# Output tiles of two channel mixers in pairs by seven block products, and a token-major end, in a two-layer hybrid trunk on one core

## The chip, the cores and the metric

The kernel runs on one core of one Trainium2 chip. The metric is the device time of one execution in microseconds (us); lower is better. Before the change it is 1336.59 us, the median of 3 runs (1335.65 to 1339.41).

## What is computed

The reference is a trunk of two layers over 512 tokens of width 1024 with 256 memory tokens. Layer 0 mixes time with a recurrence, layer 1 with attention over chunks; both add memory attention, an output projection, and then a channel mixer. At the end the stream is normalised once more. The change touches the channel mixers (`conv_glu`) and the last line:

```python
def conv_glu(h, w_in, conv_w, conv_b, w_out):
    gate, val = jnp.split(h @ w_in, 2, axis=-1)
    gp = jnp.pad(gate, ((0, 0), (CONV_W - 1, 0), (0, 0)))
    conv = conv_b + sum(conv_w[j] * gp[:, j:j + seq] for j in range(CONV_W))
    return (jax.nn.gelu(conv, approximate=False) * val) @ w_out
...
    x = x + conv_glu(rms_norm(x, ln2[layer]), ffn_in[layer], ffn_conv[layer], ffn_conv_b[layer], ffn_out[layer])
return rms_norm(x, ln_f)
```

`w_in` is 1024 by 5632, `w_out` 2816 by 1024, all in float32.

## The kernel before, in words

**Layout.** The stream lies transposed in SBUF: `xT[:, m]` is the m-th of 8 tiles of 128 features (partitions) by 512 tokens. Each float32 operand of a dense product is split into a high part of type fp32r and the rest (`whi`, `wlo` of a weight, `r1h`, `r1l` and so on of an activation), and a product is three matmuls: high by high and high by low with the same weights (lines 201 and 202), and low weights by high activations (line 206). `dense` runs all matmuls of the first two kinds, then all of the third.

**Channel mixer, in part (`ffn`).** 22 hidden tiles, each with a gate and a value output. Fourteen of them go by `seven`: the two outputs by the two token halves, with the 8 k tiles in two groups of 4, form a product of two-by-two blocks, which takes seven block products instead of eight. One block product (`prod`, lines 418, 419 and 421) is 12 matmuls of 128 by 256. The left blocks are `wv`, `w1`, `wy`, `wx` (sums and differences of weights, made on VectorE and split again); the right blocks are two plain ones (`B`) and four sums of blocks of the activations (`T`), made once per layer by `sums` and kept in `xh` (high) and `tl` (low). The eight other tiles go by `eight`: two dense products of 8 k tiles, 512 tokens wide.

**Channel mixer, out part.** A loop over the 8 output tiles m. The weights of a tile come in three pieces of 8, 7 and 7 k tiles (`load_w`, line 183: a DMA into `wraw`; line 172: the cast to `whi` on ScalarE; line 178: the rest into `wlo` on VectorE). `dense` runs 66 matmuls of 512 into one of two `psd` banks. Then VectorE multiplies by `rho`, the row of 1/rms (line 499), adds to `xT` (line 500), and `after` squares the tile, adds to `acc` and, in layer 0, writes the tile scaled and split into `r2h` and `r2l` for the next layer.

**Buffers.** `wraw` has 2, `whi` and `wlo` have 3 each. The hidden tiles 0 to 7 lie in `h_`, `l_` (`r1h`, `r1l` in layer 0; `r2h`, `r2l` in layer 1), 8 to 21 in `f3h`, `f3l`. The input of the mixer lies in the other pair, `ih`, `il`.

**The end (`finish`).** The last output tile runs in two token halves. While the second half is on TensorE, the first is finished: `norm_rho` sums squares by matmuls with a column of ones (line 251), takes the inverse root on VectorE (lines 225 to 229), spreads it over 128 columns (line 259), transposes that (line 262), copies it out (line 263), and two multiplications of 4 tiles by 256 tokens (line 1346) are stored feature-major (line 1348). The second half then goes through the same steps with nothing beside it.

**Order of the work.** A scheduler places each engine's instructions at build time, by the order of the code and when buffers come free; on the chip each engine runs its list in that order. SP issues most loads and the stores, POOL the loads that add to what is there (`accum_op`) and the loads of `xT`.

Of the kernel before, what the change touches and what calls it, by code (L numbers as in the profile page):

```python
# [18 lines left out]
P = 128  # L19
# [93 lines left out]
def trunk_kernel(ctx, tc, A, out):  # L113
# [39 lines left out]
    def ps_f(shape=(P, S)):  # L153
        return banks["F"].tile(list(shape), F32, name="psf", tag="psf")
# [8 lines left out]
    def tmp(dt=F32, shape=(P, S)):  # L163
        return banks["tmp"].tile(list(shape), dt, name="tmp", tag="tmp")
# [52 lines left out]
    def split_to(h_, l_, src):  # L217
        SC.copy(h_, src)
        V.tensor_tensor(l_, src, h_, op=ALU.subtract)  # L219
# [25 lines left out]
    def norm_rho(acc_, rho_, n=4, rc_=None):  # L245
        run(norm_steps(acc_, rho_, n, rc_))
# [103 lines left out]
    def ffn(l, hp, ih, il, h_, l_, xT, after, last=None):  # L350
# [8 lines left out]
        tl = hp.tile([P, 6, S], F32R, name="tl")  # L359

        def low(k, n):
            return tl[:, 2 * k + n] if k < 3 else (f3h, f3l)[n][:, NFF - 9]

        def high(k):
            return xh[0][:, 2 * k:2 * k + 2]

        xh = []

        def B(r, c):
            return lambda k: (ih[:, 4 * r + k, HT[c]], il[:, 4 * r + k, HT[c]])  # L370

        def T(n):
            n -= 1
            return lambda k: (high(k)[:, n // 2, HT[n % 2]], low(k, n // 2)[:, HT[n % 2]])

        def sums(k):
            u, w = tmp(), tmp()
            for t_, q in ((u, k), (w, k + 4)):
                nc.sync.dma_start(t_[:], xd[q])
                SC.activation(t_[:], t_[:], AF.Copy, scale=Vc(f"ln2_{l}", q))  # L380
            t12, t34 = tmp(), tmp()
            V.tensor_tensor(t12[:, HT[0]], u[:, HT[1]], u[:, HT[0]], op=ALU.subtract)
            V.tensor_tensor(t34[:, HT[0]], w[:, HT[1]], u[:, HT[1]], op=ALU.subtract)
            V.tensor_tensor(t12[:, HT[1]], w[:, HT[1]], t12[:, HT[0]], op=ALU.subtract)
            V.tensor_tensor(t34[:, HT[1]], w[:, HT[0]], t12[:, HT[1]], op=ALU.subtract)
            for n, t_ in enumerate((t12, t34)):
                split_to(high(k)[:, n], low(k, n), t_[:])

        def gated(j, g, v):
            c = tmp()  # L390
# [40 lines left out]
        def seven(j):  # L431
# [3 lines left out]
            nc.sync.dma_start(rg[:], A["ffn_in"][l, j, 0])  # L435
            GP.dma_start(rg[:, one], A["ffn_in"][l, j, 0][:, two], accum_op=ALU.add)
            nc.sync.dma_start(rv[:], A["ffn_in"][l, j, 1])
            wv = split_w(rv[:], 1024)
            w1 = split2(own("w1", 512), rg[:, one])
            V.tensor_tensor(rg[:, one], rg[:, one], rv[:, one], op=ALU.subtract)  # L440
# [3 lines left out]
            wx = split2(own("wx", 1024), rv[:])  # L444
            b, c = ps_d((P, 256)), ps_f((P, 256))
# [9 lines left out]
            V.tensor_tensor(v[:, HT[0]], a[:], v[:, HT[0]], op=ALU.add)  # L455
            prod(b[:], wx, 0, T(3), False)
            SC.copy(g[:, HT[1]], b[:])
# [13 lines left out]
        for j in range(NFF):  # L471
# [17 lines left out]
        for m in range(KD):  # L489
            us = []  # L490
            for lo, n in ((0, 8), (8, 7), (15, 7)):
                us.append((load_w(A["ffn_out"][l, m][:, lo * P:(lo + n) * P], n * P), list(range(lo, lo + n))))
            if m == KD - 1 and last is not None:
                last(us, hid, xT)
                break
            ps = ps_d()
            run(dense(ps[:], us, hid))
            t = tmp()
            V.tensor_tensor(t[:], ps[:], rho[:], op=ALU.mult)
            V.tensor_tensor(xT[:, m], xT[:, m], t[:], op=ALU.add)  # L500
            after(xT, m)
        return xT


# [805 lines left out]
    with ExitStack() as fctx:  # L1310
        open_banks(fctx, S=2, F=4)
        open_tmp(fctx, 6)
        hp = fctx.enter_context(tc.tile_pool(name="hpB", bufs=1))
        out_proj(1, act2, "ln2_1", r1h, r1l, xT, [0, 1, 2, 6, 7, 3, 4, 5], pre, [0, 1, 2, 6, 7, 3])
        norm_rho(acc, rho[:])

        def after(xT, m):
            norm_tile(xT[:, m], m, None, None, None)
            SC.activation(xT[:, m], xT[:, m], AF.Copy, scale=Vc("ln_f", m))


        def finish(us, hid, xT):
            m = KD - 1
            hts = (slice(0, 256), slice(256, 512))

            def half(u):
                ps = pss[u] = ps_d((P, 256))
                yield from dense(ps[:], us, lambda k: tuple(t[:, hts[u]] for t in hid(k)))

            def store(u):  # L1330
                ht = hts[u]
                x_ = xT[:, m, ht]
                t = tmp()
                V.tensor_tensor(t[:, :256], pss[u][:], rho[:, ht], op=ALU.mult)
# [4 lines left out]
                V.tensor_tensor(acc[:, ht], acc[:, ht], sq[:, :256], op=ALU.add)  # L1339
                yield 2000  # L1340
                norm_rho(acc[:, ht], rho[:, ht], 2)
                yield 4000
                for g in range(0, KD, 4):
                    o = wp.tile([P, 1024], F32, name="wraw", tag="wraw", bufs=2)
                    ov = o[:].rearrange("p (m t) -> p m t", m=4)
                    V.tensor_tensor(ov, xT[:, g:g + 4, ht], rho[:, ht].unsqueeze(1).to_broadcast([P, 4, 256]),
                                    op=ALU.mult)
                    nc.sync.dma_start(out[:, g:g + 4, ht], ov)

            pss = {}  # L1350
            run(half(0))
            weave([(half(1), 22 * 648), (store(0), 12000)])
            run(store(1))

        ffn(1, hp, r1h, r1l, r2h, r2l, xT, after, finish)


# [79 lines left out]
```

## Time and profile before

| | |
|---|---|
| median of 3 runs | 1336.59 us (1335.65 to 1339.41) |
| the profiled execution | 1334.86 us |
| its span, first to last instruction | 1333.0 us |
| out part of the mixer, layer 0 | 620.40 to 740.08 us |
| out part of the mixer, layer 1, up to its last tile | 1197.80 to 1302.50 us |
| last tile, both halves | 1302.50 to 1319.74 us |
| from the last dense matmul to the end | 13.26 us |

A row of the profile gives engine, line of the kernel, operation, the tiles written and read, and times in us unless marked ns. PE is TensorE, PEld its loads of weights, DVE VectorE, ACT ScalarE. The windows view gives the busy time of each engine in a stretch, the granted clock of TensorE (1.00 is full), and what the DMA engines moved. The chain view follows what released each step, back from the last instruction. The span differs from the time of the same execution by 1.86 us, which lie around the program.

### The profile page before, as it was taken

To read this page: it belongs to the slowest core of one execution; us is meant where nothing else is said; L and a number is where in the kernel's file an instruction comes from. 1 tells how busy PE (TensorE), PEld (TensorE's weight loads), DVE (VectorE), ACT (ScalarE), POOL (GpSimd) and SP (SyncE) were. 2 spreads that over 40 slices of the span, in tenths; PEclk is the share of its full clock that TensorE was granted. 3 is DMA by queue.
4 is the path that set the end of the run, shared out by engine and by line. 5 is a ranking of instruction groups with operands and counts; after the bars stand their busy time and mean duration, and the time that the engine had idled before them with its cause. 6 is when DMAs were issued, how large, how long until landed. Compare 5 with 4: busy or idle time off the path is not lost.

```text
span 1333.0 us, 23600 instructions
## 1 busy us (share of the span) xinstructions
PE 1292.0 (97%) x9274; PEld 1100.6 (83%) x9274; DVE 955.3 (72%) x2036; ACT 695.2 (52%) x1189; POOL 63.1 (5%) x105
## 2 busy tenths in 40 slices
PE   7989999999999999999999999999999999999996
PEld 6777777777788999998888878786889999998885
DVE  8886888877478989985443675657679998973334
ACT  6656555555346555654232576657465665642221
POOL 0000000000010000001000000000100000010000
PEclk9999999999999999999999999999999999999998
DMA  6265545463364444434333323232643444343322
GB/s 214 92 190 119 103 102 115 101 162 84 96 192 140 119 127 135 118 89 152 102 102 103 119 88 95 88 118 65 204 158 96 132 132 115 113 153 91 98 87 78
DMA packets 73088, 159.55 MB, mean 120 GB/s; under 512 B 25872, under 2 KB 30224, under 8 KB 72976
## 3 DMA queue, kind: packets, MB, share of 16 engines
q1 hardware_dynamic: 63648, 132.34, 32.2%
q0 software_dynamic: 9328, 25.70, 9.4%
q8 instruction: 73, 1.20, 0.4%
q14 instruction: 39, 0.32, 0.1%
HBM read 147.00 MB, written 11.01 MB: 119 GB/s over the span
## 4 chain that ended last, share of the span: by engine, by line
PE 82%; DVE 11%; ACT 3%; DMA 2%; issue 1%; DVEq 0%; SPq 0%; ACTq 0%
PE psd L206 11%; PE psd L201 11%; PE psd L202 11%; PE psf L201 4%; PE psf L202 4%; PE psf L206 4%; PE psd L421 4%; PE psd L419 4%; PE psd L418 4%; PE psf L421 3%; PE psf L419 3%; PE psf L418 3%; DVE Xu L799 2%; DVE Xs L801 1%; PE pss L1252 1%
## 5 line engine op out<-in xcount | busy, mean ns | idle before, releaser
L172 ACT CAST whi<-wraw 128x1024 fp32r<-128x1024 f32 (+1 forms) x174 | 178.9, 1029 | 281.5 <-DMA wraw<-in_ffn_out_dram 90.3
L178 DVE TENSOR_TENSOR wlo<-wraw,whi 128x1024 fp32r<-128x1024 f32 (+1 forms) x155 | 185.2, 1195 | 155.5 <-PE psd L206 80.9
L201 PE MATMUL psd<-r1h,whi 128*128 128x512 f32 x318 | 127.4, 401 | 0.0
L202 PE MATMUL psd<-r1l,whi 128*128 128x512 f32 x318 | 125.3, 394 | 0.0
L202 PE MATMUL psd<-f3l,whi 128*128 128x512 f32 (+1 forms) x238 | 88.6, 377 | 0.0
L201 PE MATMUL psd<-f3h,whi 128*128 128x512 f32 (+1 forms) x238 | 88.6, 377 | 0.0
L206 PE MATMUL psd<-r1h,wlo 128*128 128x512 f32 x318 | 84.9, 399 | 0.0
L201 PE MATMUL psd<-r2h,whi 128*128 128x512 f32 (+1 forms) x200 | 77.0, 389 | 0.8 <-ACT r2h L1259 0.7
L202 PE MATMUL psd<-r2l,whi 128*128 128x512 f32 (+1 forms) x200 | 76.3, 385 | 0.8 <-DVE r2l L219 0.8
L201 PEld LDWEIGHTS psd<-r1h,whi 128*128 128x128 f32 x318 | 59.9, 188 | 13.0 <-issue 0.5
L202 PEld LDWEIGHTS psd<-r1l,whi 128*128 128x128 f32 x318 | 59.8, 188 | 11.6 <-issue 0.3
L206 PEld LDWEIGHTS psd<-r1h,wlo 128*128 128x128 f32 x318 | 57.7, 188 | 12.3 <-issue 0.8
L418 PE MATMUL psd<-xh,whi 128*128 128x256 f32 x224 | 56.1, 283 | 0.0
L206 PE MATMUL psd<-f3h,wlo 128*128 128x512 f32 (+1 forms) x238 | 53.7, 377 | 0.0
L201 PEld LDWEIGHTS psd<-f3h,whi 128*128 128x128 f32 x238 | 44.8, 188 | 8.2
L202 PEld LDWEIGHTS psd<-f3l,whi 128*128 128x128 f32 x238 | 44.8, 188 | 8.2
L206 PE MATMUL psd<-r2h,wlo 128*128 128x512 f32 (+1 forms) x200 | 50.3, 385 | 0.0
L201 PE MATMUL psf<-r2h,whi 128*128 128x512 f32 x128 | 50.1, 391 | 0.0
L201 PE MATMUL psf<-r1h,whi 128*128 128x512 f32 x128 | 50.1, 391 | 0.0
L202 PE MATMUL psf<-r2l,whi 128*128 128x512 f32 x128 | 49.9, 390 | 0.0
L202 PE MATMUL psf<-r1l,whi 128*128 128x512 f32 x128 | 49.9, 390 | 0.0
L206 PEld LDWEIGHTS psd<-f3h,wlo 128*128 128x128 f32 x238 | 42.9, 188 | 8.2
(458 smaller groups left out, 3482.1 us busy)
## 6 DMA issues: line engine op xcount, KB each, us to landing
wraw<-in_ffn_in_dram SPq DMA_DIRECT2D x60, 512.0 KB, 3.8
rg<-in_ffn_in_dram SPq DMA_DIRECT2D x28, 512.0 KB, 3.4
wraw<-in_ffn_out_dram SPq DMA_DIRECT2D x32, 448.0 KB, 3.3
wraw<-in_wA_dram SPq DMA_DIRECT2D x20, 512.0 KB, 4.1
wraw<-in_w_out_dram SPq DMA_DIRECT2D x16, 512.0 KB, 4.0
wraw<-in_ffn_out_dram SPq DMA_DIRECT2D x16, 512.0 KB, 4.4
wlo<-in_wA_dram POOLq DMA_DIRECT2D x15, 512.0 KB, 8.0
rg<-in_ffn_in_dram POOLq DMA_DIRECT2D x28, 256.0 KB, 4.9
```

What stands on the lines that cost most here:

```text
L172: SC.copy(hi[:, :n], raw)
L178: V.tensor_tensor(lo[:, :n], raw, hi[:, :n], op=ALU.subtract)
L201: PE.matmul(ps, wh[:, j * P:(j + 1) * P], ah, start=start and n == 0, stop=False)
L202: PE.matmul(ps, wh[:, j * P:(j + 1) * P], al, start=False, stop=False)
L206: PE.matmul(ps, wl[:, j * P:(j + 1) * P], act(k)[0], start=False, stop=stop and n == len(ks) - 1)
L418: PE.matmul(ps, wh[:, ws], ah, start=start and k == 0, stop=False, skip_group_check=not start)
L419: PE.matmul(ps, wh[:, ws], al, start=False, stop=False, skip_group_check=not start)
L421: PE.matmul(ps, wl[:, o + k * P:o + k * P + P], a(k)[0], start=False, stop=k == 3, skip_group_check=not start)
L799: V.tensor_tensor(uv, L1.rearrange("p i o -> p o i").to_broadcast([P, k, n]), X[:, 0:k, q:q + 1].to_broadcast([P, k, n]), op=ALU.mult)
L801: V.tensor_tensor(X[:, 0:k, q + 1:], X[:, 0:k, q + 1:], uv, op=ALU.add)
L1252: PE.matmul(pso[HS[hh], kt * P:], vS[i // 2][:, kt, (i % 2 * 2 + hh) * 64:(i % 2 * 2 + hh + 1) * 64], pts[hh][:, kt, kt * P:], start=kt == ...
```

## The change

The out part becomes a list of steps. In layer 0 these are `single(0)`, `single(1)`, `both(2)`, `both(4)`, `both(6)`; in layer 1 the last two tiles stay `single(6)` and `single(7)`. So five pairs of output tiles are formed in a new way: `both(m)` runs k tiles 8 to 21 of each of the two tiles as before (42 matmuls of 512), and k tiles 0 to 7 of both together by the seven block products of `seven`, with the hidden tiles 0 to 7 in the place of the input. The left blocks are made by `operands`, the code cut out of `seven`. Two of the seven products are added into the bank `d0` of the first tile, five go through two `psf` banks into two tiles `s0`, `s1`, which are added to the dense sums before the multiplication by `rho`.

The four sums `T` of the hidden tiles are made during the first two single tiles (`four`, lines 388 to 391, from `h_ + l_`, line 567) and stored where the input of the mixer lay, in tiles 3 to 7 of `ih` and `il`, and in `tl`. In layer 0 this is where the next layer's split tiles go, so the split of tiles 3 to 7 (`after`) comes after the products of the last pair.

At the end the first token half is as before, but for the layout of its store. For the second half the scaled tiles are transposed on TensorE into four `psf` banks (`turn`, line 1436), tokens on partitions; the squares of the last tile go to TensorE by themselves, without the addition to `acc` (lines 1441 and 1450); the inverse root stays one number per partition, and VectorE and ScalarE each scale two banks out (line 1464 and the one above), each followed by a store of 128 by 512. The output array becomes two halves, put together on the host.

```diff
+        def both(m):
+            full = [A["ffn_out"][l, m + u] for u in range(2)]
+            u0 = pieces(m, ((8, 7), (15, 7)))
+            wv, w1, wy, wx = operands(full[1][:, :1024], full[0][:, :1024])
+            yield
+            d0 = ps_d()
+            run(dense(d0[:], u0, hid))
+            b, c = ps_f((P, 256)), ps_f((P, 256))
+            s0, s1 = tmp(), tmp()
+            prod(b[:], wv, 0, H(0, 0))
+            SC.copy(s0[:, HT[0]], b[:])
+            prod(c[:], w1, 0, T(1))
+            prod(b[:], wy, 0, T(2), False)
+            SC.copy(s0[:, HT[1]], b[:])
+            V.tensor_tensor(s0[:, HT[1]], c[:], s0[:, HT[1]], op=ALU.add)
+            prod(d0[:, HT[0]], wv, 512, H(1, 0), False)
+            prod(b[:], wx, 0, T(3), False)
+            SC.copy(s1[:, HT[1]], b[:])
+            V.tensor_tensor(s1[:, HT[1]], c[:], s1[:, HT[1]], op=ALU.add)
+            prod(b[:], wy, 512, T(4), False)
+            SC.copy(s1[:, HT[0]], b[:])
+            prod(d0[:, HT[1]], wx, 512, H(1, 1), False)
+            u1 = pieces(m + 1, ((8, 7), (15, 7)))
+            yield
+            arrive(m, d0, s0)
+            d1 = ps_d()
+            run(dense(d1[:], u1, hid))
+            arrive(m + 1, d1, s1)
...
+        out_at[0] = [t[:, q] for t in (ih, il) for q in range(3, 8)]
+        for n, st in enumerate(steps):
+            next(st, None)
+            if n < 2:
+                for k in range(2 * n, 2 * n + 2):
+                    u, w = tmp(), tmp()
+                    for t_, q in ((u, k), (w, k + 4)):
+                        V.tensor_tensor(t_[:], h_[:, q], l_[:, q], op=ALU.add)
+                    four(k, u, w)
+            if n + 1 < len(steps):
+                next(steps[n + 1])
...
+            older(0)
+            for m_ in range(5):
+                turn(m_)
+            sq = arrive(1)
+            for t in range(2):
+                if t:
+                    older(t)
+                PE.matmul(ps[:, 2 * t:2 * t + 2], sq[:, t * P:t * P + P], C("ones_d"), start=False, stop=True)
+            for m_ in range(5, m):
+                turn(m_)
+            a = cp.tile([P, 8], F32, name="rha", tag="rha")
+            V.tensor_scalar(a[:, :2], ps[:, 0:4:2], RMS_EPS, None, op0=ALU.add)
+            r = rsqrt_small(cp, a[:, :2], 2)
+            turn(m)
+            for g in range(2):
+                o = wp.tile([P, 1024], F32, name="whi", tag="whi")
+                for t in range(2):
+                    o_ = o[:, t * S:t * S + S]
+                    if t:
+                        SC.activation(o_, pt[t][g][:], AF.Copy, scale=r[:, t:t + 1])
+                    else:
+                        V.tensor_scalar(o_, pt[t][g][:], r[:, t:t + 1], None, op0=ALU.mult)
+                    nc.sync.dma_start(out[1][:, t * 1024 + g * S:t * 1024 + g * S + S], o_)
```

TensorE in layer 1 of before, the start of output tile 5: it begins with the hidden tiles 0 to 7 (`r2h`, `r2l`), 512 wide, behind the low weights of tile 4.

```order
4881 L206 MATMUL psd<-r2h,wlo 128x512 x8
4882 L206 MATMUL psd<-f3h,wlo 128x512 x14
4883 L201 MATMUL psd<-r2h,whi 128x512
4884 L202 MATMUL psd<-r2l,whi 128x512
4885 L201 MATMUL psd<-r2h,whi 128x512
```

TensorE at the same place of the changed kernel, inside the products of tiles 4 and 5: the end of the fifth product (`wx` by a sum, into the `psf` bank b), the first four matmuls of the seventh (`wx` by `r2`, into d0 in `psd`), and the start of the sixth (`wy`, lying in a `whi` buffer, into b again).

```order
5044 L427 MATMUL psf<-r1h,wxl 128x256 x2
5045 L427 MATMUL psf<-r1l,wxl 128x256 x2
5046 L424 MATMUL psd<-r2h,wxh 128x256
5047 L425 MATMUL psd<-r2l,wxh 128x256
5048 L424 MATMUL psd<-r2h,wxh 128x256
5049 L425 MATMUL psd<-r2l,wxh 128x256
5050 L424 MATMUL psf<-r1h,whi 128x256
5051 L425 MATMUL psf<-tl,whi 128x256
```

The hidden tiles 0 to 7 have left the dense part of each of the two tiles; 84 matmuls of 256 stand for 48 of 512, and between the fifth and the sixth product, which both write b, stand four matmuls that do not.

VectorE in layer 0 of before, from the multiplication by `rho` of tile 1 on (the `wlo` rows split the pieces of the following tiles).

```order
1196 L499 TENSOR_TENSOR tmp<-psd,rho 128x512
1197 L500 TENSOR_TENSOR xT<-xT,tmp 128x512
1198 L178 TENSOR_TENSOR wlo<-wraw,whi 128x896
1199 L237 TENSOR_TENSOR acc<-acc,tmp 128x512
1200 L243 SCALAR_TENSOR_TENSOR r2l<-xT,vec,r2h 128x512
1201 L178 TENSOR_TENSOR wlo<-wraw,whi 128x1024
```

VectorE of the changed kernel, from the multiplication by `rho` of tile 1 on: the making of the left blocks of the first pair. The first `wlo` is the low part of `wv`, `wxl` that of `wx`, and the `wlo` from `rg` that of `wy`.

```order
1226 L511 TENSOR_TENSOR tmp<-psd,rho 128x512
1227 L512 TENSOR_TENSOR xT<-xT,tmp 128x512
1228 L446 TENSOR_TENSOR rg<-rg,wraw 128x512
1229 L178 TENSOR_TENSOR wlo<-wraw,whi 128x1024
1230 L237 TENSOR_TENSOR acc<-acc,tmp 128x512
1231 L448 TENSOR_TENSOR wraw<-rg 128x512
1232 L449 TENSOR_TENSOR wraw<-wraw,rg 128x512
1233 L243 SCALAR_TENSOR_TENSOR r2l<-xT,vec,r2h 128x512
1234 L219 TENSOR_TENSOR wxl<-wraw,wxh 128x1024
1235 L178 TENSOR_TENSOR wlo<-rg,whi 128x1024
```

Three subtractions and three splits of the left blocks stand where one or two splits of pieces stood, and the low part of `wy` comes last among them.

TensorE at the end of before, behind the low weights of the second token half.

```order
5068 L206 MATMUL psd<-f3h,wlo 128x256 x14
5069 L251 MATMUL pss<-cst,acc 128x2 x2
5070 L262 MATMUL pss<-cst,tmp 128x128 x2
5071 L1432 UNCONDITIONAL_BRANCH
```

TensorE at the end of the changed kernel (`tmp` holds the squares of the last tile; line 1436 is the transposition of `xT`).

```order
5233 L206 MATMUL psd<-f3h,wlo 128x256 x14
5234 L1441 MATMUL pss<-cst,acc 128x2
5235 L1436 MATMUL psf<-cst,xT 128x128 x12
5236 L1450 MATMUL pss<-cst,tmp 128x2
5237 L1441 MATMUL pss<-cst,acc 128x2
5238 L1450 MATMUL pss<-cst,tmp 128x2
5239 L1436 MATMUL psf<-cst,xT 128x128 x4
5240 L1544 UNCONDITIONAL_BRANCH
```

Twelve transpositions of tiles that are ready stand ahead of the matmuls that wait for the squares, four behind them, and the transposition of the spread inverse root is gone.

More of the change, by code (lines that the diff above doesn't have):

```diff
@@ L361, in low, with high, B @@
         def low(k, n):
-            return tl[:, 2 * k + n] if k < 3 else (f3h, f3l)[n][:, NFF - 9]
-        def high(k):
-            return xh[0][:, 2 * k:2 * k + 2]
+            if k < 3:
+                return tl[:, 2 * k + n]
+            return (f3h, f3l)[n][:, NFF - 9] if out_at[0] is None else out_at[0][8 + n]
+        def high(k, n):
+            return xh[0][:, 2 * k + n] if out_at[0] is None else out_at[0][2 * k + n]
+        out_at = [None]
         xh = []
-        def B(r, c):
-            return lambda k: (ih[:, 4 * r + k, HT[c]], il[:, 4 * r + k, HT[c]])
+        def B(r, c, a=(ih, il)):
+            return lambda k: tuple(t[:, 4 * r + k, HT[c]] for t in a)
         def T(n):
             n -= 1
-            return lambda k: (high(k)[:, n // 2, HT[n % 2]], low(k, n // 2)[:, HT[n % 2]])
+            return lambda k: (high(k, n // 2)[:, HT[n % 2]], low(k, n // 2)[:, HT[n % 2]])
         def sums(k):
@@ L386, in sums @@
             for n, t_ in enumerate((t12, t34)):
-                split_to(high(k)[:, n], low(k, n), t_[:])
+                split_to(high(k, n), low(k, n), t_[:])
         def gated(j, g, v):
@@ L429, in split2, with operands @@
             return w
-        def seven(j):
+        def operands(src_g, src_v):
             rv = wp.tile([P, 1024], F32, name="wraw", tag="wraw", bufs=2)
@@ L434, in seven @@
             one, two = slice(0, 512), slice(512, 1024)
-            nc.sync.dma_start(rg[:], A["ffn_in"][l, j, 0])
-            GP.dma_start(rg[:, one], A["ffn_in"][l, j, 0][:, two], accum_op=ALU.add)
-            nc.sync.dma_start(rv[:], A["ffn_in"][l, j, 1])
+            nc.sync.dma_start(rg[:], src_g)
+            GP.dma_start(rg[:, one], src_g[:, two], accum_op=ALU.add)
+            nc.sync.dma_start(rv[:], src_v)
             wv = split_w(rv[:], 1024)
@@ L444, in seven @@
             wx = split2(own("wx", 1024), rv[:])
+            return wv, w1, wy, wx
+        def seven(j):
+            wv, w1, wy, wx = operands(A["ffn_in"][l, j, 0], A["ffn_in"][l, j, 1])
             b, c = ps_d((P, 256)), ps_f((P, 256))
@@ L488, in ffn, with H, pieces @@
                     GP.dma_start(xT[:, m], xd[m])
[L489 to L492, printed above, removed]
+        def H(r, c):
+            return B(r, c, (h_, l_))
+        def pieces(m, cuts):
+            return [(load_w(A["ffn_out"][l, m][:, lo * P:(lo + n) * P], n * P), list(range(lo, lo + n)))
+                    for lo, n in cuts]
@@ new lines, in arrive, with single @@
+        def arrive(m, ps, part=None):
+            t = tmp()
+            if part is not None:
+                V.tensor_tensor(part[:], ps[:], part[:], op=ALU.add)
+                ps = part
+            V.tensor_tensor(t[:], ps[:], rho[:], op=ALU.mult)
+            V.tensor_tensor(xT[:, m], xT[:, m], t[:], op=ALU.add)
+            norm_tile(xT[:, m], m, None, None, None)
+            if m < 3 or last is not None:
+                after(xT, m)
+        def single(m):
+            yield
+            us = pieces(m, ((0, 8), (8, 7), (15, 7)))
@@ L493, in ffn @@
             if m == KD - 1 and last is not None:
                 last(us, hid, xT)
-                break
+                return
             ps = ps_d()
             run(dense(ps[:], us, hid))
[L498 to L501, printed above, removed]
+            yield
+            arrive(m, ps)
+        def both(m):
+            full = [A["ffn_out"][l, m + u] for u in range(2)]
+            u0 = pieces(m, ((8, 7), (15, 7)))
+            wv, w1, wy, wx = operands(full[1][:, :1024], full[0][:, :1024])
+            yield
+            d0 = ps_d()
[16 more added lines that the diff above has]
+            u1 = pieces(m + 1, ((8, 7), (15, 7)))
+            yield
+            arrive(m, d0, s0)
+            d1 = ps_d()
+            run(dense(d1[:], u1, hid))
+            arrive(m + 1, d1, s1)
@@ new lines, in ffn @@
+        steps = [single(0), single(1), both(2), both(4)]
+        steps += [both(6)] if last is None else [single(6), single(7)]
+        next(steps[0])
+        out_at[0] = [t[:, q] for t in (ih, il) for q in range(3, 8)]
[6 more added lines that the diff above has]
+                        V.tensor_tensor(t_[:], h_[:, q], l_[:, q], op=ALU.add)
+                    four(k, u, w)
+            if n + 1 < len(steps):
+                next(steps[n + 1])
+            elif last is None:
+                for m in range(3, 6):
+                    after(xT, m)
+            run(st)
@@ L502, in ffn @@
+        if last is None:
+            for m in range(6, KD):
+                after(xT, m)
         return xT
@@ L1323, in finish, with arrive @@
             m = KD - 1
-            hts = (slice(0, 256), slice(256, 512))
+            pss = {}
             def half(u):
                 ps = pss[u] = ps_d((P, 256))
[L1328 to L1332, printed above, removed]
+                yield from dense(ps[:], us, lambda k: tuple(t[:, HT[u]] for t in hid(k)))
+            def arrive(u):
+                x_ = xT[:, m, HT[u]]
                 t = tmp()
-                V.tensor_tensor(t[:, :256], pss[u][:], rho[:, ht], op=ALU.mult)
+                V.tensor_tensor(t[:, :256], pss[u][:], rho[:, HT[u]], op=ALU.mult)
                 V.tensor_tensor(x_, x_, t[:, :256], op=ALU.add)
@@ L1338, in store @@
                 SC.activation(x_, x_, AF.Copy, scale=Vc("ln_f", m))
-                V.tensor_tensor(acc[:, ht], acc[:, ht], sq[:, :256], op=ALU.add)
+                return sq
+            def store():
+                sq = arrive(0)
+                V.tensor_tensor(acc[:, HT[0]], acc[:, HT[0]], sq[:, :256], op=ALU.add)
                 yield 2000
-                norm_rho(acc[:, ht], rho[:, ht], 2)
+                norm_rho(acc[:, HT[0]], rho[:, HT[0]], 2)
                 yield 4000
@@ L1345, in store, with turn, older @@
                     ov = o[:].rearrange("p (m t) -> p m t", m=4)
-                    V.tensor_tensor(ov, xT[:, g:g + 4, ht], rho[:, ht].unsqueeze(1).to_broadcast([P, 4, 256]),
+                    V.tensor_tensor(ov, xT[:, g:g + 4, HT[0]], rho[:, HT[0]].unsqueeze(1).to_broadcast([P, 4, 256]),
                                     op=ALU.mult)
-                    nc.sync.dma_start(out[:, g:g + 4, ht], ov)
-            pss = {}
+                    nc.sync.dma_start(out[0][:, g * 256:(g + 4) * 256], o[:])
             run(half(0))
-            weave([(half(1), 22 * 648), (store(0), 12000)])
-            run(store(1))
+            weave([(half(1), 22 * 648), (store(), 12000)])
+            toks = [slice(256 + t * P, 256 + t * P + P) for t in range(2)]
+            pt = [[ps_f() for g in range(2)] for t in range(2)]
+            def turn(m_):
+                for t in range(2):
+                    PE.transpose(pt[t][m_ // 4][:, m_ % 4 * P:m_ % 4 * P + P], xT[:, m_, toks[t]], C("ident"))
+            ps = ps_s()
+            def older(t):
+                PE.matmul(ps[:, 2 * t:2 * t + 2], acc[:, toks[t]], C("ones_d"), start=True, stop=False)
+            older(0)
[14 more added lines that the diff above has]
+                o = wp.tile([P, 1024], F32, name="whi", tag="whi")
+                for t in range(2):
+                    o_ = o[:, t * S:t * S + S]
[4 more added lines that the diff above has]
+                    nc.sync.dma_start(out[1][:, t * 1024 + g * S:t * 1024 + g * S + S], o_)
         ffn(1, hp, r1h, r1l, r2h, r2l, xT, after, finish)
@@ L1435 @@
     got = r.results[0]["out_0_dram"]
-    return np.ascontiguousarray(got.transpose(2, 1, 0).reshape(1, S, KD * P))
+    first = got[0].reshape(P, KD, 256).transpose(2, 1, 0).reshape(256, KD * P)
+    last = got[1].reshape(P, 2, KD * P).transpose(1, 0, 2).reshape(256, KD * P)
+    return np.ascontiguousarray(np.concatenate([first, last])[None])
```

6 lines of the change are left out of this document (3 added, 3 removed).

## Prediction

> **What bounds the kernel now.** I read the page's busy times first, then the windows of the two stages that the change touches.
>
> ```profile
> PE 1292.0 (97%) x9274; PEld 1100.6 (83%) x9274; DVE 955.3 (72%) x2036; ACT 695.2 (52%) x1189; POOL 63.1 (5%) x105
> 620.40:740.08 119.68, 119.68 (x529) 99.10 (x529) 48.16 (x57) 35.72 (x45) 0.00 (x0) 1.00 0.32 93
> 1197.80:1302.50 104.70, 104.70 (x464) 86.69 (x464) 36.39 (x40) 28.71 (x35) 0.00 (x0) 1.00 0.32 94
> ```
>
> In a row of windows stand the length, then the busy time of PE, PEld, DVE, ACT and POOL, the granted clock and the DMA share. TensorE is busy through all of both stages at full clock; VectorE has 48.16 of 119.68 us and 36.39 of 104.70 to do, ScalarE less. So TensorE bounds them, and a matmul taken out there shortens the kernel as long as the other engines keep up. Next the chain of waits, for the pace of both kinds of matmul: the low weights of two output tiles that follow each other, and the ends of block products in the in part.
>
> ```profile
> 1207.77 4.99 PE psd L206 x22
> 1222.73 4.99 PE psd L206 x22
> ...
> 1167.67 0.48 PE psd L421 x4
> 1169.11 0.48 PE psf L421 x4
> 1177.75 0.48 PE psf L421 x4
> ```
>
> One output tile takes 1222.73 - 1207.77 = 14.96 us for 66 matmuls of 512, 0.2267 us each. One block product takes 1.44 us for 12 matmuls of 256, 0.120 us each; from the first to the last of these rows are seven products, 10.08 us, with no gap between them. The end of the chain, after the last dense matmul:
>
> ```profile
> 1317.09 2.65 PE psd L206 x22
> ...
> 1321.13 0.44 DVE acc L1339
> ...
> 1321.71 0.59 PE pss L251 x4
> ...
> 1322.32 0.17 DVE rha L253
> ...
> 1324.29 0.17 DVE rsq L229
> ...
> 1324.92 0.68 PE pss L262 x2
> ...
> 1326.03 1.23 DVE wraw L1346
> 1327.25 1.13 DVEq L1432
> ```
>
> Nothing is beside this: from 1319.74 to 1333.0 every step waits for the one before, and the stores come last.
>
> **The change part by part.** The seven products take out two times 24 matmuls of 512 and put in 84 of 256. Out go 48 x 0.2267 = 10.88 us, in come 84 x 0.120 = 10.08: 0.80 us less per pair, 4.0 us for five.
>
> The Trainium skill, "TensorE: Matmul & The Clock Gate", section "Back-to-back issue gap", gives N/2.4 + 2.5 ns for one matmul that follows another at full clock, 109.2 ns at 256 columns and 215.8 at 512. By it a pair would save 48 x 215.8 - 84 x 109.2 ns = 1.19 us, five pairs 5.9. The rows above have 120 and 226.7 ns, both some 11 ns over it, and 84 matmuls carry that more often than 48; the rows decide.
>
> Between the fifth and the sixth product ScalarE must copy the bank b out, and only four matmuls (0.48 us) stand between. No row of before has this case; the nearest is a bank that is copied out and refilled with nothing between (the projection of v, then the group of the copy used here):
>
> ```profile
> 757.82 0.28 PE L1202 MATMUL psd<-whi,r1h 128*128 128x256 f32 x1
> 758.04 0.47 ACT L1206 ACTIVATE vS<-psd,rc 128x256 f32<-128x256 f32 x1
> 758.57 0.38 PE L1202 MATMUL psd<-whi,r1h 128*128 128x256 f32 x1 [0.47 <-ACT vS L1206]
> ...
> L457 ACT COPY tmp<-psd 128x256 f32<-128x256 f32 x14 | 5.1, 366 | 2.9 <-PE psd L421 2.8
> ```
>
> From the last matmul's start to the next lie 0.75 us with a copy of 0.47, so 0.65 with one of 0.366. The matmul itself and four more take 0.60. That leaves 0.05 us idle per pair, 0.25 in all; the ends are 0 (the copy hides) and 0.8 per pair (rival B). The other copies of b have a whole product of 1.44 us as cover.
>
> The left blocks and the sums add work on VectorE and ScalarE. I price it with these groups, and with the end of the last gate of layer 1:
>
> ```profile
> L178 DVE TENSOR_TENSOR wlo<-wraw,whi 128x1024 fp32r<-128x1024 f32 x29 | 35.5, 1224 | 60.8 <-PE psd L206 55.0 <-ACT whi L172 5.7
> L178 DVE TENSOR_TENSOR wlo<-wraw,whi 128x896 fp32r<-128x896 f32 x15 | 16.4, 1091 | 9.1 <-ACT whi L172 6.6 <-PE psd L206 2.5
> L440 DVE TENSOR_TENSOR rg<-rg,wraw 128x512 f32<-128x512 f32 x13 | 9.0, 690 | 0.3
> L455 DVE TENSOR_TENSOR tmp<-psf,tmp 128x256 f32<-128x256 f32 x14 | 5.9, 419 | 0.4 <-PE psf L421 0.4
> L499 DVE TENSOR_TENSOR tmp<-psd,rho 128x512 f32<-128x512 f32 x7 | 4.8, 692 | 3.1 <-PE psd L206 3.1
> ...
> 1200.38 0.68 DVE L219 TENSOR_TENSOR f3l<-tmp,f3h 128x512 fp32r<-128x512 f32 x1
> ...
> L172 ACT CAST whi<-wraw 128x1024 fp32r<-128x1024 f32 (+1 forms) x174 | 178.9, 1029 | 281.5 <-DMA wraw<-in_ffn_out_dram 90.3
> ...
> wraw<-in_ffn_in_dram SPq DMA_DIRECT2D x60, 512.0 KB, 3.8
> wraw<-in_ffn_out_dram SPq DMA_DIRECT2D x32, 448.0 KB, 3.3
> ```
>
> A pair needs on VectorE four pieces (4 x 1.09), the splits of `wv`, `wy`, `wx` (3 x 1.22) and `w1` (0.69), three subtractions (2.07) and the additions of s0, s1 (2 x 0.42 + 2 x 0.69): 13.0 us where two tiles took 2 x (1.22 + 2 x 1.09) = 6.8. The sums of a layer are 16 operations of 512 (8 additions, 8 splits) and 16 of 256: 11.0 + 6.7 = 17.7 us. Layer 0 comes to 48.2 + 3 x 6.2 + 17.7 = 84.5 of some 117 us, layer 1 to 36.4 + 2 x 6.2 + 17.7 = 66.5 of 103. ScalarE gets about 3 us per pair and 5 per layer. The totals fit; what counts is the order.
>
> The tightest place is the first pair of layer 0, whose left blocks stand behind all the sums. Put t = 0 at the start of tile 0. The last gate ends at 1201.06 - 1197.80 = 3.3 in layer 1, and I take the same here; three rows of the sums (1.8) go ahead of it, so it ends at 5.1. Down VectorE's list: the other rows of the first sums end at 12.1; two splits for tile 1 at 14.5; the multiplication waits for tile 0's end at 14.96; with the second sums, the third piece and tile 0's addition and split the list stands at 28. The two pieces of the pair end at 30.2. The load of `wv` needs the buffer that the first of them frees at 29.2, and lands 3.8 later, at 33.0. The subtraction, the split of `wv`, the addition to `acc`, two subtractions, the split for the next layer, `wx` and `wy` take 7.2 us, and two waits for ScalarE's casts of about 1 us, partly hidden, some 0.7 more; `wy` low is last, at 40.9. TensorE needs it in the third product after the high weights, at 2 x 14.96 + 42 x 0.2267 + 2 x 1.44 + 0.96 = 43.3. So 2.4 us are to spare here, and the load costs nothing; without that cover each us more is a us on the path. In a later pair `wy` low must wait for a `wlo` buffer, free after the first seven low matmuls of the pair's first tile, 7.9 us into that tile's 9.5; split at 9.2, it is needed at 9.5 + 3.8 = 13.3: 4 us spare.
>
> SP's loads keep their order, and the loads into `rg` stand ahead of some for `wraw`; they wait for buffers that are free before those. POOL's adding loads for the first two pairs stand ahead of the loads of `xT`, which wait for the last product of the in part anyway. The granted clock is 1.00 in both stages and stays.
>
> At the end of layer 0 the splits of tiles 6 and 7 come late. In before the next stage loses this much on TensorE:
>
> ```profile
> 740.08:754.13 14.05, 12.66 (x61) 9.71 (x60) 11.38 (x26) 5.33 (x7) 0.43 (x3) 1.00 0.66 202
> ```
>
> 1.4 us of 14.05 are idle, waiting for `rho`. VectorE has one addition more on that path (0.69) and fewer splits in front of it, as seven of those for the next stage move ahead into the last dense part. I take 0, and bounds of 1.0 gained and 0.7 lost.
>
> The end of the program: the squares of the last half are ready at 1321.11 as before. TensorE has by then two rows of sums (0.59/4 bounds one at 0.15, eight in 0.84 at another place make it 0.11) and twelve transpositions:
>
> ```profile
> 745.24 0.84 PE pss L251 x8
> 777.17 0.65 PE pss L1238 x6
> ```
>
> 0.2 + 12 x 0.11 = 1.5 us after 1319.74, so 1321.27; no later than the squares plus the issue (1321.25). Six rows follow instead of four, 0.8 for 0.59, and the root starts at 1322.09 where it started at 1322.32: 0.2 us gained, with 0.44 for the addition to `acc` in it. The root keeps its length and ended at 1324.46. From there to the first store before were the spreading, two transpositions, a copy and a multiplication of 1.23, to 1327.25: 2.79 us. Now it is one eviction of 128 by 512 on VectorE, by L499 0.69 with 0.02 of issue, ScalarE doing another beside it: 2.07 gained. And the stores:
>
> ```profile
> 1322.00:1324.00 2.00, 0.28 (x3) 0.20 (x2) 1.40 (x9) 0.00 (x0) 0.00 (x0) 0.96 0.00 0
> 1326.00:1328.15 2.15, 0.00 (x0) 0.00 (x0) 2.12 (x2) 0.00 (x0) 0.00 (x0) 0.50 0.00 0
> 1328.15:1331.28 3.13, 0.00 (x0) 0.00 (x0) 0.23 (x1) 0.00 (x0) 0.00 (x0) 0.50 0.99 333
> 1331.28:1333.00 1.72, 0.00 (x0) 0.00 (x0) 0.00 (x0) 0.00 (x0) 0.00 (x0) 0.50 0.01 3
> ```
>
> The granted clock falls only after 1322, when TensorE's part of the new end is all but over (1322.09 and four transpositions). The megabyte moves from 0.90 us after the first store is released, for 3.13 us at a DMA share of 0.99, and 1.72 us follow. So the first store sets the end. Four quarters are 0.78 us of transfer each, and released within 0.7 us of the first they keep the queue full. The end gains 0.2 + 2.07 = 2.3 us; ends: 3.0 (the wider rows go faster, the root starts at once) and, below, a loss of 0.4 (rival D).
>
> Sum: -4.0 + 0.25 + 0 - 2.3 = -6.05 us. Against the profiled execution, 1334.86, that is 1328.8; it lies 1.73 under the median of the runs, and I take the difference from the median: 1336.59 - 6.05 = 1330.5.
>
> **The rivals.** B: each border between products costs a little, since b is passed back and forth, and the pairs save nothing: 0.8 us, 0.13 at each of six borders. For it: b is written five times in a row of seven products, and nothing of another tile is woven in. Against it: the 10.08 us above without a gap. Time: 1336.59 - 2.3 = 1334.3.
>
> C, the slower one: `wy` low is late at every pair, because it stands last on VectorE behind `wx`, whose cast waits for ScalarE, and the load behind a buffer. If it comes L us later than I count, TensorE stands L - 2.4 us per pair. At 3.6 the whole gain is gone, at 4.4 the kernel is slower by 4 us. One more load in the line (3.8) with its cast and split (2.2) makes L = 6: 5 x 3.6 - 6.05 = +12, 1348.5. For it: the order above, and two `wraw` buffers, one of them held by `wv` until `wx` is made. Against: the 4 us spare in later pairs.
>
> D: every store of the end pays its own 0.90 us before data moves; three more are 2.7, and the end loses 0.4: 1336.59 - 3.75 + 0.4 = 1333.2. Against: the second store of before does not show in the 0.99.
>
> E: a short matmul takes half of a long one, 0.1134, and a pair saves 10.88 - 9.52 = 1.36 us: 6.8 - 0.25 + 2.3 gives 1327.7. Against: 0.120 in the seven products shown. By the Trainium skill's gap it would be 5.9 in the place of 6.8, 1328.6.
>
> That the change does not do what it says is excluded by the order: the products and the transpositions are there.
>
> **How the numbers follow.** About 0.3% of the time, 4.0 us, is what a measurement can tell from no change. Forecast 0.72, B 0.10, C 0.05, D 0.07, E 0.06. The forecast's own range is its terms' bounds, and 1 us for the runs' spread: 1328 to 1333; 0.04 of it lies above 1332.6. So faster 0.68 + 0.06 = 0.74, the same 0.04 + 0.10 + 0.07 = 0.21, slower 0.05. The range to hold 8 in 10 takes in E at its lower end and most of D, half of B: 1327.6 to 1334.0.
>
> **What would show it.** Right: windows of the stages with TensorE busy throughout; a pair in 29.1 to 29.2 us where two tiles took 29.92; an idle of at most 0.1 before the sixth product, released by the copy of b (line 545); 10.9 to 11.0 us from the last dense matmul to the end where there were 13.26. Wrong: idle time of PE on `wlo` or `wy` in the third product (C), on copies at every border (B), gaps in the DMA share between the four stores (D), or transpositions that end after the squares.

## The result, and the profile after

The median of six runs is 1329.95 us (1327.31 to 1332.23), beside 1337.26 us (1333.47 to 1339.41) for six runs of the kernel before: a ratio of 0.9943 with a 95% interval of 0.9923 to 0.9963. That is 7.3 us less, with an interval of 4.9 to 10.3. The forecast was 1330.5. The six runs spread over 4.9 us, so that the two numbers lie so close says less than the stages below.

The profiled execution of after took 1332.23 us with a span of 1330.4, only 2.6 below the profiled one of before. It comes to layer 0's out part 3.85 us later, though TensorE's matmuls up to there are the same and in the same order, so the two traces are compared by stages and not by their ends. First the page's row of engines, then windows of the stages (length, then PE, PEld, DVE, ACT and POOL, granted clock, DMA share).

```profile
PE 1293.9 (97%) x9472; PEld 1109.8 (83%) x9472; DVE 1013.8 (76%) x2143; ACT 718.9 (54%) x1236; POOL 67.6 (5%) x110
```

```profile
624.24:742.30 118.06, 118.06 (x637) 102.51 (x637) 81.68 (x116) 49.41 (x73) 0.89 (x1) 1.00 0.32 93
742.30:754.82 12.52, 12.52 (x61) 9.81 (x60) 9.18 (x22) 4.91 (x8) 0.43 (x3) 1.00 0.54 184
1198.89:1319.62 120.73, 120.57 (x675) 105.54 (x674) 70.26 (x109) 41.73 (x60) 0.00 (x0) 1.00 0.27 80
60.00:120.00 60.00, 54.68 (x474) 47.32 (x475) 45.29 (x119) 32.04 (x53) 3.62 (x4) 0.91 0.61 157
```

In the first and third row, the out parts of layer 0 and layer 1, TensorE works at full clock, all but 0.16 us of the time, though VectorE went from 48.16 to 81.68 us in the first. The second row is the boundary behind layer 0: 14.05 us with 12.66 of TensorE's work before, 12.52 now, with no idle that the window shows. In the last row, far ahead of the change, the granted clock is 0.91; the trace of before has 0.97 in the same window.

To compare runs I cut each trace at five instructions: the first matmul of layer 0's out part, the first matmul behind that part, the first of v's projection, the first of layer 1's out part, and the end of the last dense matmul. The timeline puts the boundary's first matmul 0.16 us ahead of the moment at which the chain of waits lets it begin, so the boundary reads 14.22 and 12.68 here. All in us, with the kernels of the experiments below:

| kernel | start of out part 0 | out part 0 | boundary | up to out part 1 | out part 1 | end |
|---|---|---|---|---|---|---|
| before | 620.23 | 119.68 | 14.22 | 443.50 | 122.11 | 13.26 |
| after | 624.08 | 118.06 | 12.68 | 443.90 | 120.90 | 10.78 |
| e1_swap | 625.55 | 117.34 | 12.70 | 443.62 | 120.42 | 10.87 |
| e2_end_only | 624.05 | 119.68 | 14.14 | 443.46 | 122.11 | 10.86 |
| e3_pairs_only | 621.49 | 118.04 | 12.71 | 443.78 | 120.89 | 13.29 |
| e4_last_single | 624.46 | 118.60 | 13.93 | 443.48 | 120.91 | 10.82 |
| e6_before_r1_early | 622.28 | 119.68 | 13.12 | 443.27 | 122.12 | 13.33 |
| e5_pad4 | 621.85 | 118.30 | 12.68 | 443.39 | 120.91 | 10.87 |
| e5_pad7 | 622.78 | 119.19 | 12.68 | 443.46 | 121.88 | 10.81 |

Out parts with the same code agree within 0.02 us, boundaries and ends within 0.1. The first and the fourth column are the same work in every kernel, and they spread over 5.3 and 0.6 us: there the runs differ, which is why a median leaves 2 to 3 us of doubt where a stage leaves 0.1. By stages the change is worth -1.62 - 1.54 - 1.21 - 2.48 = -6.85 us, well inside the interval of the medians.

Now the places that the prediction named. In the chain of waits, the low weights of the first product in each of layer 0's pairs (start, length, what):

```profile
664.63 0.48 PE psf L427 x4
...
694.01 0.48 PE psf L427 x4
...
723.39 0.48 PE psf L427 x4
```

A pair takes 29.38 us, against 29.92 before and 29.1 to 29.2 in the forecast. The difference lies between the fifth and the sixth product. The timeline there, TensorE and then ScalarE:

```profile
670.47 0.40 PE L427 MATMUL psf<-r2l,wxl 128*128 128x256 f32 x2
670.71 0.28 PE L424 MATMUL psd<-r1h,wxh 128*128 128x256 f32 x1
670.83 0.28 PE L425 MATMUL psd<-r1l,wxh 128*128 128x256 f32 x1
670.95 0.28 PE L424 MATMUL psd<-r1h,wxh 128*128 128x256 f32 x1
671.07 0.28 PE L425 MATMUL psd<-r1l,wxh 128*128 128x256 f32 x1
671.33 0.39 PE L424 MATMUL psf<-r2h,whi 128*128 128x256 f32 x1
671.56 0.28 PE L425 MATMUL psf<-tl,whi 128*128 128x256 f32 x1
...
670.91 0.37 ACT L545 COPY tmp<-psf 128x256 f32<-128x256 f32 x1 [0.94 <-PE psf L427]
```

The fifth product's last matmul starts at 670.59, the copy at 670.91, and the sixth product at 671.33 where the spacing of 0.12 would have put it at 671.19: 0.14 of wait. Then the next matmul follows after 0.22 to 0.23 instead of 0.12, some 0.10 more. No view of waits lists this stall; it shows only in the starts. It stands at this border in all five pairs and at no other.

The end, in the chain:

```profile
1316.98 2.64 PE psd L206 x22
...
1319.74 1.37 PE psf L1436 x12
1321.12 0.32 PE pss L1450 x2
...
1321.92 0.17 DVE rha L1454
...
1323.88 0.17 DVE rsq L229
...
1324.07 0.75 DVE whi L1464
1324.82 0.66 DVEq L1544
```

What TensorE's matmuls on the squares waited for there:

```profile
PEld pss L1450 <- ACT tmp L1411: 0.2, 1, 0.2
```

The last of the twelve transpositions starts at 1320.84, the squares are done at 1321.00, and the first matmul on them starts at 1321.05, so the transpositions hold nothing up. The root starts 2.30 us after the last dense matmul (2.58 before), the first store is released 2.90 after that (4.93 before), and 5.58 remain (5.75 before). The stores in windows:

```profile
1324.80:1325.70 0.90, 0.00 (x0) 0.00 (x0) 0.68 (x2) 0.60 (x2) 0.00 (x0) 0.89 0.04 14
1325.70:1328.85 3.15, 0.00 (x0) 0.00 (x0) 0.00 (x0) 0.00 (x0) 0.00 (x0) 0.50 0.93 329
1328.85:1330.40 1.55, 0.00 (x0) 0.00 (x0) 0.00 (x0) 0.00 (x0) 0.00 (x0) 0.50 0.00 0
```

Four stores run as one transfer: 0.90 us of lead-in once, then a DMA share of 0.93.

### The profile page after: what moved, and what is told of

Its sections match the earlier page's. It is cut to its first block, busy times and chain, and to the rows that moved or that the text cites. A ratio compares the mean times of both kernels' runs of the same rounds, so it can differ in the third digit from the quotient of the medians.

```text
span 1330.4 us, 24187 instructions
## 1 busy us (share of the span) xinstructions
PE 1293.9 (97%) x9472; PEld 1109.8 (83%) x9472; DVE 1013.8 (76%) x2143; ACT 718.9 (54%) x1236; POOL 67.6 (5%) x110
## 3 DMA queue, kind: packets, MB, share of 16 engines
q8 instruction: 74, 1.21, 0.4%
## 4 chain that ended last, share of the span: by engine, by line
PE 82%; DVE 10%; ACT 3%; DMA 3%; issue 2%; SPq 0%; DVEq 0%; ACTq 0%; POOLq 0%
PE psd L201 9%; PE psd L202 9%; PE psd L206 9%; PE psd L424 4%; PE psd L427 4%; PE psd L425 4%; PE psf L201 4%; PE psf L202 4%; PE psf L206 4%; PE psf L424 4%; PE psf L427 4%; PE psf L425 4%; DVE Xu L875 2%; DVE Xs L877 1%; PE pss L1328 1%
## 5 line engine op out<-in xcount | busy, mean ns | idle before, releaser
L178 DVE TENSOR_TENSOR wlo<-wraw,whi 128x1024 fp32r<-128x1024 f32 (+1 forms) x150 | 178.8, 1192 | 79.9 <-ACT whi L172 37.7
L201 PE MATMUL psd<-r1h,whi 128*128 128x512 f32 x270 | 109.0, 404 | 0.9 <-DVE xT L344 0.9
L202 PE MATMUL psd<-r1l,whi 128*128 128x512 f32 x270 | 106.9, 396 | 0.0
L206 PE MATMUL psd<-r1h,wlo 128*128 128x512 f32 x270 | 74.1, 405 | 0.0
L201 PE MATMUL psd<-r2h,whi 128*128 128x512 f32 (+1 forms) x168 | 64.6, 389 | 0.8 <-ACT r2h L1335 0.7
L202 PE MATMUL psd<-r2l,whi 128*128 128x512 f32 (+1 forms) x168 | 63.9, 384 | 0.8 <-DVE r2l L219 0.8
L201 PEld LDWEIGHTS psd<-r1h,whi 128*128 128x128 f32 x270 | 50.8, 188 | 12.4 <-issue 1.8
L202 PEld LDWEIGHTS psd<-r1l,whi 128*128 128x128 f32 x270 | 51.0, 189 | 9.7 <-issue 0.3
L206 PEld LDWEIGHTS psd<-r1h,wlo 128*128 128x128 f32 x270 | 49.6, 191 | 10.6 <-issue 0.7
L218 ACT CAST wxh<-wraw 128x1024 fp32r<-128x1024 f32 x33 | 34.4, 1044 | 20.2 <-DVE wraw L449 17.5
```

The costliest lines, as they stand in the source:

```text
L178: V.tensor_tensor(lo[:, :n], raw, hi[:, :n], op=ALU.subtract)
L201: PE.matmul(ps, wh[:, j * P:(j + 1) * P], ah, start=start and n == 0, stop=False)
L202: PE.matmul(ps, wh[:, j * P:(j + 1) * P], al, start=False, stop=False)
L206: PE.matmul(ps, wl[:, j * P:(j + 1) * P], act(k)[0], start=False, stop=stop and n == len(ks) - 1)
```

## The experiments

The expectations were written before each run. The theory: a pair saves exactly its difference in matmuls and loses 0.25 to the copy of b; the boundary gains because r1 is free early; the new end gains 2.5 by itself; and wy low has some 4 us to spare. e4_last_single, e5_pad4 and e5_pad7 ran once each, so only their stages are read here.

**e1_swap: the seventh product as cover for the copy.**

```diff
+            prod(d0[:, HT[1]], wx, 512, H(1, 1), False)
             prod(b[:], wy, 512, T(4), False)
             SC.copy(s1[:, HT[0]], b[:])
-            prod(d0[:, HT[1]], wx, 512, H(1, 1), False)
```

> The seventh product of each pair is moved whole ahead of the sixth, so that twelve matmuls of 256 (1.44 us) stand between the fifth product and the sixth, where four stood. In the trace of the changed kernel the copy of b starts 0.32 us after the start of the fifth product's last matmul, takes 0.37, and the sixth product's second matmul follows its first by 0.23 instead of 0.12: 0.25 us per pair that the count of matmuls does not have. Theory (the copy makes the stall): the sixth product starts without a wait, a pair of layer 0 goes from 29.38 to 29.1 us, layer 0's out part from 118.06 to 117.3, the whole kernel about 1.2 us faster than the changed kernel. Rival (the 0.25 belongs to reading and refilling the same bank, or to the products as such, and not to what stands between): a pair stays at 29.3 to 29.4 us.

Measured: out part 0 in 117.34 us, out part 1 in 120.42, that is 0.24 per pair less than after in both. The chain (first product's low weights in two pairs) and the timeline at the start of the sixth product:

```profile
666.10 0.48 PE psf L427 x4
...
695.24 0.48 PE psf L427 x4
```

```profile
673.02 0.28 PE L425 MATMUL psd<-r1l,wxh 128*128 128x256 f32 x1
673.14 0.64 PE L427 MATMUL psd<-r1h,wxl 128*128 128x256 f32 x4
673.62 0.28 PE L424 MATMUL psf<-r2h,whi 128*128 128x256 f32 x1
673.74 0.28 PE L425 MATMUL psf<-tl,whi 128*128 128x256 f32 x1
```

A pair takes 29.14 us, and all starts are 0.12 apart: the wait is gone and so is the late start behind it. So what stands between is the cause, as the theory had it. Without the stall five pairs save (119.68 - 117.34) + (122.11 - 120.42) = 4.03 us, where the count of matmuls gave 4.0. The estimate of 5.9 in the prediction goes by the Trainium skill, "TensorE: Matmul & The Clock Gate", section "Back-to-back issue gap", which gives its formula for an isolated gap; the measurement decides. The medians, 1331.88 of ten runs against 1337.39 for before, a ratio of 0.9953 (0.9934 to 0.9971), don't tell this kernel from after, which has 0.9943; by its two out parts it is 1.2 us ahead of after.

**e2_end_only and e3_pairs_only: the two halves of the change.** One is before with the new `finish` and the two-part output array, the other is after with the old ones:

```diff
-            weave([(half(1), 22 * 648), (store(), 12000)])
-            toks = [slice(256 + t * P, 256 + t * P + P) for t in range(2)]
...
+            weave([(half(1), 22 * 648), (store(0), 12000)])
+            run(store(1))
```

> The kernel before, with the new token-major end alone. Theory: the stages stay as before (119.7 us for layer 0's out part, 14.0 for the boundary), and from the last dense matmul to the end it is 10.8 us where it was 13.26: 2.5 us less in all. Rival (the end owes part of its gain to what the pairs leave behind on VectorE and ScalarE): 11.5 to 13.

> The five pairs alone, with the old end. Theory: layer 0's out part 118.1 us, the boundary to the next stage 12.5, layer 1's two pairs 29.4 each, the end 13.3: about 4.4 us less than before. Rival (the boundary's 1.5 us are chance and change from run to run): boundary 13.5 to 14.1, 2.9 us less than before.

Measured: the end alone leaves every stage and takes 10.86 us; the pairs alone have 118.04, 12.71 (12.55 by the chain, as the expectation counts) and 120.89, and an end of 13.29. The medians are 1335.95 (ratio 0.9982, 0.9964 to 1.0) and 1334.17 (0.9975, 0.9955 to 0.9994). Both theories hold, and by the stages the parts add up, 2.40 and 4.37 us to 6.77 where after has 6.85; the medians are too rough to show it. The end owes nothing to the pairs, and the boundary's gain belongs to the pairs.

**e4_last_single: layer 0's last two tiles one by one.**

```diff
-        steps += [both(6)] if last is None else [single(6), single(7)]
+        steps += [single(6), single(7)]
```

> The changed kernel, but layer 0's last two output tiles are done one by one as before; its first four stay pairs, and the order of the splits for the next stage is still free to move. Theory (the boundary gains because r1 is read last by the seventh product of the last pair, 9 us before the part ends, so that the seven splits into r1 are over when the last tile's sums arrive): with single tiles r1 is read up to the last tile's low weights, the splits come after again, and the boundary goes back from 12.5 us to about 14; layer 0's out part is 118.6 with its two pairs. Rival (the boundary gains from the scaled splits being taken out of the tiles' ends, pairs or not): boundary stays at 12.5.

Measured: out part 0 in 118.60 us, one pair's 0.54 more, and the boundary at 13.93, so 1.25 of the 1.54 us are lost again. TensorE's waits in the boundary (for what, us in total, times, longest):

```profile
PE psd L1278 <- DVE tmp L1240: 0.9, 1, 0.9
PE pss L262 <- DVE tmp L259: 0.2, 1, 0.2
```

VectorE's list there is like that of before again: the seven splits into r1 run until 743.99 (the last three shown), 0.9 us into the boundary, and two splits of weights stand between the steps of the root (the second of them shown).

```profile
741.92 2.07 DVE L243 SCALAR_TENSOR_TENSOR r1l<-xT,vec,r1h 128x512 fp32r<-128x512 f32 x3
...
752.94 0.16 DVE L228 SCALAR_TENSOR_TENSOR rsq<-rsq,rha 128x4 f32<-128x4 f32 x1
753.05 1.23 DVE L178 TENSOR_TENSOR wlo<-wraw,whi 128x1024 fp32r<-128x1024 f32 x1
754.19 0.15 DVE L229 SCALAR_TENSOR_TENSOR rsq<-rsq,rsq 128x4 f32<-128x4 f32 x1
```

The root in before, with the first of its two splits:

```profile
747.65 0.16 DVE L227 TENSOR_TENSOR rsq<-rsq 128x4 f32<-128x4 f32 x1
747.99 1.23 DVE L178 TENSOR_TENSOR wlo<-wraw,whi 128x1024 fp32r<-128x1024 f32 x1 [0.18 <-ACT whi L172]
749.13 0.15 DVE L228 SCALAR_TENSOR_TENSOR rsq<-rsq,rha 128x4 f32<-128x4 f32 x1
```

In after the seven splits into r1 end at 739.97, before the boundary, the ten steps of the root stand in one piece, and `wlo` comes behind them:

```profile
748.76 0.16 DVE L225 TENSOR_SCALAR rsq<-rha 128x4 int32<-128x4 int32 x1
...
750.54 0.16 DVE L229 SCALAR_TENSOR_TENSOR rsq<-rsq,rsq 128x4 f32<-128x4 f32 x1
750.93 1.23 DVE L178 TENSOR_TENSOR wlo<-wraw,whi 128x1024 fp32r<-128x1024 f32 x1 [0.24 <-PE psd L206]
```

So the last pair, and not the move of the splits in the text, makes most of the difference at the boundary.

**e6_before_r1_early: r1 free early without any pair.**

```diff
-            run(dense(ps[:], us, hid))
+            if m == KD - 1:
+                run(dense(ps[:], us[:1], hid, stop=False))
+                run(dense(ps[:], us[1:], hid, start=False))
+            else:
+                run(dense(ps[:], us, hid))
```

> The kernel before, with one change of order: the last output tile of layer 0 does the 24 matmuls on k tiles 0 to 7 first, high and low, and then the 42 of the rest, so that r1 is free some 9.5 us before the tile ends. No block products. Theory (r1 being free early is what shortens the boundary): from the last dense matmul to the projection of v it is 12.5 us where it was 14.05, and the kernel gains 1.5 us. Rival (the pairs shorten it in another way): 14.0, no gain.

Measured: boundary 13.12 us, between the two. The waits and the window:

```profile
PE psd L201 <- ACT r2h L242: 0.5, 1, 0.5
```

```profile
741.96:755.08 13.12, 12.58 (x61) 10.19 (x60) 9.77 (x23) 6.38 (x9) 0.43 (x3) 1.00 0.52 174
```

Both waits for the root are gone, as the theory says: r1 free early is enough for that, without a block product. A new wait of 0.54 has come in, for ScalarE's scaled copy of the last tile, at which after does not stand; with it away the boundary would be 12.58, an estimate from the window's busy time. The theory holds for the cause and was 0.5 off in the size. The whole kernel's ratio, 0.9987 (0.9969 to 1.0004), is inconclusive.

**e5_pad4 and e5_pad7: wy low made late.** Subtractions whose result is written over stand ahead of the split of `wy`'s low weights, four in every pair, or seven in all pairs but layer 0's last:

```diff
         SC.copy(hi[:, :n], raw)
+        for _ in range(pad):
+            V.tensor_tensor(lo[:, :512], raw[:, :512], raw[:, 512:1024], op=ALU.subtract)
```

> The changed kernel with four more subtractions of 128 by 512 on VectorE (0.60 us each from start to start) ahead of the split of wy's low weights in each of the five pairs; their results are written over by that split. By VectorE's order one split of a piece (1.02) moves ahead of it too, so wy low is ready 3.4 us later. In the changed kernel's trace it is ready at 663.36 and needed at 667.52 in the first pair, at 692.74 and 696.9 in the second. Theory (4.1 us are to spare): TensorE doesn't stand, every pair stays at 29.4 us, the kernel as fast as the changed one. Rival (the slack is smaller than the trace makes it, because something else on VectorE goes late with it): 1 us or more of idle in each third product, 5 us in all.

> The same with seven subtractions, in four pairs (not in layer 0's last). By VectorE's order the split of a piece (1.02) and, in three of the pairs, that of w1 (0.60) move ahead of wy's: ready at 662.13 + 3 x 0.60 + 1.02 + 3 x 0.60 + 0.60 + 0.60 + 1.23 = 669.2 where 667.52 is needed. Theory: TensorE stands 1.6 to 1.8 us in the third product of those pairs and about 1.0 in layer 1's second pair, which has w1 behind; 6 us slower than the changed kernel. Rival (other work hides it, the products' order on TensorE is not what waits): under 2 us in all.

Measured with four: out part 1 unchanged (120.91), out part 0 longer by 0.24, all of it in its last pair, where a split into r1 stood in the row as well. In the first pair wy low was ready at 664.90, 3.46 after the first product began; it is needed 3.84 after, and nothing waited. The theory holds in four pairs of five. With seven the cost was 1.13 in layer 0 and 0.98 in layer 1, 2.1 us where 6 were expected; out part 0's first pair, VectorE and then TensorE:

```profile
661.07 2.14 DVE L174 TENSOR_TENSOR wlo<-rg 128x512 fp32r<-128x512 f32 x3
663.13 1.08 DVE L180 TENSOR_TENSOR wlo<-wraw,whi 128x896 fp32r<-128x896 f32 x1
664.13 2.14 DVE L174 TENSOR_TENSOR wlo<-rg 128x512 fp32r<-128x512 f32 x3
666.18 0.69 DVE L221 TENSOR_TENSOR w1l<-rg,w1h 128x512 fp32r<-128x512 f32 x1
666.79 0.68 DVE L174 TENSOR_TENSOR wlo<-rg 128x512 fp32r<-128x512 f32 x1
667.50 1.23 DVE L180 TENSOR_TENSOR wlo<-rg,whi 128x1024 fp32r<-128x1024 f32 x1
```

```profile
666.05 0.28 PE L426 MATMUL psd<-r1h,whi 128*128 128x256 f32 x1
...
668.21 0.28 PE L426 MATMUL psd<-r1h,wxh 128*128 128x256 f32 x1
668.78 0.62 PE L429 MATMUL psf<-r2h,wlo 128*128 128x256 f32 x3 [0.29 <-DVE wlo L180]
```

wy low is ready at 668.73, where the third product could have used it at 666.05: 2.7 us late. But between stand 19 matmuls of the fourth and the seventh product (`psd`, from 666.05), which the program writes behind it. The scheduler, which makes the order at build time, now has them ahead, and the row counts only 0.29 of wait (0.45 by the starts); the rest of this pair's loss lies at the borders of b, which have less cover now. The theory falls for this kernel: lateness that the scheduler knows of is filled with other products. What a late load that it doesn't foresee would cost wasn't tried.

## Why the prediction was right, and where it was not

The time was right (1330.5 against 1329.95), in part by luck: two of its terms were wrong by 0.95 and 1.54 us in opposite directions.

- **The difference in matmuls, 0.80 per pair.** Right: e1_swap shows 4.03 us for five pairs.
- **"That leaves 0.05 us idle per pair, 0.25 in all."** This step was mis-sized: 0.24 per pair, 1.2 in all, inside its stated ends of 0 and 0.8. The row from before was misread. It puts the copy 0.22 us behind the start of the matmul at 757.82, but that matmul belongs to another group. The copy's own group had ended with the matmul at 756.98, and the copy started when ScalarE was done with the cast ahead of it, at 758.02. The next copy of that stage had no such cast ahead and stood waiting; it starts 0.32 us behind its last matmul, as in after:

```profile
757.40 0.62 ACT L1183 CAST ks<-tmp 64x512 fp32r<-64x512 f32 x1
...
761.42 0.28 PE L1204 MATMUL psd<-wlo,r1h 128*128 128x256 f32 x1
...
761.75 0.47 ACT L1206 ACTIVATE vS<-psd,rc 128x256 f32<-128x256 f32 x1 [3.23 <-PE psd L1204]
```

With 0.32, a copy of 0.37 and 0.05 to the next matmul the sum is 0.74, less 0.60 for five matmuls: 0.14, the wait that after has. The late start behind the stall, some 0.10 us more, was left out, though before has it at the same place (758.57 to 758.79).

- **"I take 0, and bounds of 1.0 gained and 0.7 lost" for the boundary.** This is the step that failed: 1.54 us gained, outside the bounds. The text had the cause in hand, that seven splits move ahead into the last dense part, but set them off against one more addition and stopped. The row quoted there says what is to be had: 1.4 us idle waiting for `rho`. When the splits go, `rho` has an uninterrupted root ahead of it, and the idle goes whole (e4_last_single brings it back, e6_before_r1_early removes the waits for the root without a pair); the other 0.14 is a smaller busy time of TensorE, and what made that smaller stays open.
- **wy low, "2.4 us are to spare".** Right that the load costs nothing, and 1.8 too careful: it was ready 39.1 us after tile 0's start instead of 40.9. The first of the pair's two pieces was split by 27.9, not 29.2, so the buffer came free and `wv` landed earlier. "Without that cover each us more is a us on the path" did not hold where the scheduler knew of the lateness, by e5_pad7.
- **The end, 2.3.** Right, 2.48: 0.28 before the root (0.2 forecast), 2.03 to the first store (2.07), 0.17 in the stores (0).
- **Rivals.** B (0.8 lost per pair) falls: 0.24 is lost, at one border and not at six. C falls: no stage has a wait on `wlo` or `wy`. D falls by the windows of the stores. E falls by e1_swap, which has 0.80 and not 1.36. The forecast's sum of -6.05 became -6.85: +0.92 in the pairs (0.95 more at the stall, 0.03 more saved), -1.54 at the boundary, -0.18 at the end.

## What to carry to other kernels

Where a bank is copied out and refilled, put a whole product between: four matmuls (0.48 us) left 0.24 us per pair here, twelve (1.44) left nothing. By the sum of 0.74 us above six would do, an estimate that no run tried. Before a row is taken as a model of a wait, look at what the copying engine did just ahead of it. Where a stage starts with an idle wait, ask what the change takes out of the list of the engine that is waited for; the idle already in the trace is the size of what can be won. And when runs spread by some us, cut the traces at a few instructions: stages of the same code agreed within 0.1 us here.

## What the runs showed of the hardware

A matmul of 256 that follows a stalled one starts 0.22 to 0.23 us after it, not 0.12 (671.33 to 671.56 in after, 758.57 to 758.79 in before), so each stall costs some 0.10 on top of the wait. From the start of a group's last matmul of 256 to a copy by ScalarE that stands waiting for it lie 0.32 us in both kernels (670.59 to 670.91, 761.42 to 761.75). The code ahead of layer 0's out part ended between 620.23 and 625.55 in nine traces; the granted clock in the window of 60 to 120 us goes with part of that (0.97 with 620.23, 0.91 with 624.08), but not with all (0.94 with 621.85 and with 624.46).
